# Cross attention queries of two heads as seven block products, beside the next head's keys and values

## The chip, the cores and the metric

The kernel runs on one core of a Trainium2 chip. The metric is the device time of one execution in microseconds (us); the time given for a kernel is the median of its runs.

## The reference

A decoder trunk of two layers over 512 tokens of width 1024, in float32. Each layer is a half-step SwiGLU FFN, a token mixer (differential attention in layer 0, a causal pooling mixer in layer 1), a cross attention of 4 heads into 256 memory tokens, and another half-step FFN; a layer norm follows each. The change touches the cross attention and the end of the pooling mixer.

```python
def memory_cross_attention(x, mem, wq, wkv, wo):      # x (1,512,1024), mem (1,256,1024)
    q = (x @ wq).reshape(B, S, XA_HEADS, XA_HEAD_DIM)  # 4 heads of 256
    k, v = jnp.split(mem @ wkv, 2, axis=-1)
    ...
    s = jnp.einsum('bshd,bmhd->bhsm', q, k).astype(jnp.float32) * (XA_HEAD_DIM ** -0.5)
    p = jax.nn.softmax(s, axis=-1).astype(v.dtype)
    o = jnp.einsum('bhsm,bmhd->bshd', p, v).reshape(B, S, D_MODEL)
    return o @ wo
...
x = layer_norm(a * x + memory_cross_attention(x, mem, xa_wq[i], xa_wkv[i], xa_wo[i]), ...)
```

## The kernel before

**Arithmetic.** Every float32 operand of a matmul is split into a high half (a rounded copy, `split`, line 114, on ScalarE = ACT) and a low half (operand minus high half, line 115, on VectorE = DVE, which so waits for ACT). One product is then three matmuls, `mm3` at lines 201 to 203: high by high, high by low, low by high. Weight tiles of 512 KB arrive by DMA issued on SyncE (SP) into a raw tile and are split into `wh` and `wl` in pieces of 128x1024; a raw tile may be loaded or added to again only when its two halves are made.

**FFN.** `up` computes its products two by two as seven block products in place of eight (a Strassen form): factors of x are made once by `second_factors` (lines 579 to 617), and the sums of weight blocks are made by DMAs that add into the raw tile in SBUF (`more`, line 636, `accum_op=ALU.add`, issued on GpSimd = POOL). Several units run in lanes, so that the additions to the tiles of one lane land while the others compute; between two uses of a raw tile stands one addition.

**Cross attention before.** `xa_main` goes head by head: keys `pk` and values `pv` of the head (`xa_kv`, 96 matmuls of 256 columns, results split into four tiles of the tag `kv`), then its queries `xq`: 48 matmuls of 512 columns (8 blocks of the inner dimension, two halves of the head's 256 columns, 3 matmuls each), 384 in the whole kernel. The raw weights are plain loads. `xa_side` (scores `xs`, softmax at lines 1290 to 1298, transposes, weighted sum `xo`, tile `oT`) is woven in by `weave`, 3 us of product time behind the head's queries. After that `to_tokens` multiplies by `wo` (`ps`) and adds into the rows X of the four token tiles, with the layer norm of each token tile: `ln_add` line 397, mean line 406 (DVE), square 419 (ACT), variance and reciprocal root `var`, `rstd` lines 420 and 421 (POOL), lines 423 and 425 (DVE), and then the transposes `pt` of its rows at line 479 (PE) with their split into `xh`, `xl`.

**Before the cross attention of layer 1** stands the pooling mixer: banded products `pp`, split into `pooled`, then `ps` and the layer norm. Beside it keys and values of head 0, after it those of head 1, are computed (`early_kv`), so that TensorE (PE) has work while the last token tiles are normalized.

**Order.** Each engine takes its instructions in a fixed order; a tile scheduler writes that order from the program and the priorities. An instruction that waits holds up what stands behind it on its engine. A DMA that POOL issues waits on POOL for the raw tile to be free.

Of the kernel before, what the change touches and what calls it, by code (L numbers as in the profile page):

```python
# [17 lines left out]
P = 128  # L18
D = 1024
S = 512  # L20
# [73 lines left out]
    return {"ident": ident, "mask": mask, "rope": rope, "band": band}  # L94


WAIT = object()


def drain(units):  # L100
    for _ in units:
        pass


class Trunk:
# [56 lines left out]
    @contextmanager  # L162
    def stage_pools(self, w, raw, order):

        with ExitStack() as ctx:
            self.stage = {}
            for n in order:
                if n == order[0]:
                    self.to_w(ctx)
                if n == "mem":  # L170
                    self.to_x(ctx)
                self.stage[n] = ctx.enter_context(self.pool(n))
            self.banks = {n: ctx.enter_context(self.pool(n, space=PSUM)) for n in ("px", "py", "yz")}
            self.w_bufs, self.raw_bufs, self.aux_turn = w, raw, 0
            self.w_order, self.raw_order = [("wh", "wl")], ["raw"]
            self.w_turn = self.raw_turn = 0
            yield
# [6 lines left out]

    def aux(self, name, tag=None):
        if tag is None:
            tag = list(self.banks)[self.aux_turn % 3]
            self.aux_turn += 1
        return self.banks[tag].tile([P, S], F32, tag=tag, name=name, bufs=2)

# [264 lines left out]
    def turn(self, t, half, two_pass=None):  # L455

        pt = self.aux("pt", "px" if "ra" in self.stage else None).rearrange("p (c n) -> p c n", c=4)
        c0 = half * S
        with self.behind() if self.last_mm else nullcontext():
            self.transpose4(pt, [self.X[t][:, c0 + j * P : c0 + (j + 1) * P] for j in range(4)])  # L460
        o = slice(t * P, (t + 1) * P)
        if self.ln_next == "ffn":
# [687 lines left out]
    def pool_mixer(self, layer, ln):  # L1150
# [32 lines left out]
            pooled.append(q)  # L1183
            yield
        wg = self.halves_wide(self.pool_w, "we", "we")
        self.w_order = [("wh", "wl")] * 3 + [("we", "we")] * 2
        self.raw_order = ["rawe"] * 3 + ["raw"] * 2
        self.begin_ln(layer, ln, 1.0)
        for t in range(NT):
            o = slice(t * P, (t + 1) * P)  # L1190
            for half in range(2):
# [12 lines left out]
                        )  # L1204
                self.ln_add(t, half, ALPHA, ps)
                yield
            self.turn_late()
            self.ln_token(t)


# [35 lines left out]
        for i, d in enumerate(self.kept):  # L1246
            self.nc.gpsimd.dma_start(self.mem_tile(2 * i), d)

    def xa_kv(self, w, h, ahead=None):
        nc = self.nc  # L1250
        rk = ahead or self.load_cols(w, h * 256)
        ps = self.mm("pk").rearrange("p (c n) -> p c n", c=2)
        for j in range(2):
            wk = rk[j] if ahead else self.halves(rk[j])
            for k in range(KC):
# [3 lines left out]
        kv = lambda: tuple(  # L1259
            self.kvp.tile([P, 2, MEM], F32R, tag="kv", name="kv", bufs=8) for _ in range(2)  # L1260
        )
        kt = kv()
        self.turn_late()
        self.split(kt[0], kt[1], ps)
        wv = self.halves_wide(self.load_wide(w, D + h * 256))
        ps = self.mm("pv").rearrange("p (m n) -> p m n", m=2)
        for m in range(2):
            o = slice(m * P, (m + 1) * P)
            for k in range(KC):
                mt = self.memT[k]  # L1270
                yield self.mm3(ps[:, m], (mt[0][:, o], mt[1][:, o]), wv[k], k == 0, k == KC - 1)
        v = kv()
        self.split(v[0], v[1], ps)
        return kt, v

    def xa_head(self, qs, kt, v):
        nc = self.nc
        pT = [self.pair("pT") for _ in range(2)]
        ps = []
        for tt in range(0, NT, 2):  # L1280
            sc = self.aux("xs").rearrange("p (t n) -> p t n", t=2)
            for i in range(2):
                o = slice((tt + i) * P, (tt + i + 1) * P)
                for c in range(2):
                    q = qs[c]
                    self.mm3(
                        sc[:, i], (q[0][:, o], q[1][:, o]), (kt[0][:, c], kt[1][:, c]), c == 0, c == 1
                    )
            mx, sm, rc = self.small("mx"), self.small("sm"), self.small("rx")
            nc.vector.tensor_reduce(mx, sc, AX.X, ALU.max, negate=True)  # L1290
# [10 lines left out]
        for tt in range(0, NT, 2):  # L1301
            p = ps[tt // 2]
            pt = self.aux("pt").rearrange("p (m i n) -> p m i n", m=2, i=2)
            for m in range(2):
                for i in range(2):
                    nc.tensor.transpose(pt[:, m, i], p[:, i, m * P : (m + 1) * P], self.ident)
            for m in range(2):
                o = slice(tt * P, (tt + 2) * P)
                self.split(pT[m][0][:, o], pT[m][1][:, o], pt[:, m].rearrange("p i n -> p (i n)"))
            yield  # L1310
        for c in range(2):
# [4 lines left out]
            o = self.pair("oT")  # L1316
            self.split(o[0], o[1], po)
            self.oT.append(o)
            yield

    def early_kv(self, layer, heads, ahead=None):
        for h in heads:
            self.kv.append((yield from self.xa_kv(self.a["xa_wkv"][layer], h, ahead)))

    def xa_main(self, layer):
        wq, wkv = self.a["xa_wq"][layer], self.a["xa_wkv"][layer]
        early = len(self.kv)
        for h in range(XA_H):
            if h >= len(self.kv):
                self.kv.append((yield from self.xa_kv(wkv, h)))  # L1330
            kt, v = self.kv[h]
            qs = []
            ws = [self.halves(lo) for lo in self.load_cols(wq, h * 256)]
            ps = [self.mm("xq") for c in range(2)]
            for p in ((0, 2 * P), (2 * P, S)) if self.late else ((0, S),):
                for c in range(2):
                    yield from self.project(ps[c], ws[c], (p,))
                    self.turn_late(1 - c)
            for c in range(2):
                q = self.pair("q")  # L1340
                self.split_scaled(q[0], q[1], ps[c], (D // XA_H) ** -0.5)
                qs.append(q)
            self.heads.append((self.clock, (qs, kt, v)))
            if 0 < early and h + early < XA_H:
                self.kv.append((yield from self.xa_kv(wkv, h + early)))
        yield from self.to_tokens(self.oT, self.a["xa_wo"][layer], 0, 4, True, False, ALPHA)

    def xa_side(self):
        for h in range(XA_H):
            while h >= len(self.heads) or self.clock < self.heads[h][0] + 3000:  # L1350
                yield WAIT
            yield from self.xa_head(*self.heads[h][1])

    def cross_attention(self, layer, ln):
        bufs = dict(q=8, oT=10, gb=2)
        if layer == 0:
            self.kv = []
            mem = self.side_pool("mem")
            with self.other_pools():
                self.stage["mem"] = mem  # L1360
                with self.phase_pool(("gb", "gb"), "p", pT=6, p=4, kv=8, _x=0, **bufs):
                    self.kvp = self.phase["kv"]
                    self.mem_tiles = []
                    with self.tc.high_priority():
                        self.turn_memory("p")
                    self.xa(layer, ln)
            self.close_side()
        else:
            with self.later, self.phase_pool(("gb", "gb"), "p", pT=6, p=4, **bufs):
                self.xa(layer, ln)  # L1370

    def xa(self, layer, ln):
        self.heads, self.oT = [], []
        self.weave(self.xa_main(layer), self.xa_side(), 2500)
        if layer == 0:
            self.keep_memory()
        self.begin_ln(layer, ln, 1.0)
        kv = lambda: tuple(self.kvp.tile([P, S], F32R, tag="kv", name="kv", bufs=8) for _ in range(2))
        homes = [[lambda: self.pair("q")] * 4, [kv] * 4]
        drain(self.to_tokens(self.oT[4:], self.a["xa_wo"][layer], 4, 4, False, True, ALPHA, homes))  # L1380


# [68 lines left out]
    def mixer(self, layer, ln):  # L1451
# [5 lines left out]
        else:  # L1457
            w = self.a["xa_wkv"][layer]
            self.later = ExitStack()
            self.later.enter_context(self.late_pools())  # L1460
            self.kvp = self.later.enter_context(self.pool("kv"))
            with self.phase_pool(("pooled", "pooled"), "sq", pooled=20, sq=1):
# [57 lines left out]
```

## Time and profile before

| | us |
|---|---|
| time, median of 3 runs | 1949.34 (1948.71 to 1950.73) |
| profiled execution, own time | 1952.38 |
| its span | 1950.6 |
| PE busy | 1918.7 (98%), 13052 matmuls |
| PE's weight loads busy | 1746.2 (90%) |
| DVE busy | 1560.5 (80%) |
| ACT busy | 1012.7 (52%) |
| POOL busy | 336.1 (17%) |
| cross attention of layer 0, on PE | 601.5 to 765.1 |
| pooling mixer and cross attention of layer 1, on PE | 1421.2 to 1614.5 |

The profiled execution took 1.8 us more than its span, and 3.0 us more than the median. In the timeline a row is start, duration, engine, line, operation, tile written, tiles read, shape and count; in square brackets the idle time before it and what ended that. Matmuls are pipelined: the distance of two starts is the pace, not the duration of one. PEclk is the share of TensorE's full clock that was granted.

### The profile page before, as it was taken

How to read it: one execution, taken by the hardware profiler on the slowest of the kernel's cores; microseconds unless marked ns; L12 is line 12 of the kernel's file. 1: busy time of each engine (PE TensorE's matmuls, PEld its weight loads, DVE VectorE, ACT ScalarE, POOL GpSimd, SP SyncE). 2: the span in 40 equal slices, each digit the busy share in tenths (PEclk: the TensorE clock that was granted, in tenths of full speed). 3: DMA queues.
4: the chain of work that ended last, by engine and by line, in shares of the span. 5: the costliest groups of instructions: out<-in, count | busy, mean ns of one | idle time of the engine just before them, and what ended most of it. 6: DMA issues, size and time to landing. Idle time of an engine off the chain costs nothing.

```text
span 1950.6 us, 32439 instructions
## 1 busy us (share of the span) xinstructions
PE 1918.7 (98%) x13052; PEld 1746.2 (90%) x13052; DVE 1560.5 (80%) x2200; ACT 1012.7 (52%) x1537; POOL 336.1 (17%) x317
## 2 busy tenths in 40 slices
PE   9999999999999999999999999999999999999998
PEld 8999998888778888989998999999888889999996
DVE  7988987788867557798887888888876468888886
ACT  6555553466655444555554555455445436555552
POOL 3212121111211002312210322112110013111211
PEclk9999999999999999999999999999999999999999
DMA  9888772322135325977695598778435336778861
GB/s 253 197 174 180 167 152 66 90 65 87 44 108 177 126 65 141 218 171 147 149 200 143 105 210 173 174 162 163 153 119 162 109 87 116 189 172 172 182 143 44
DMA packets 254182, 280.58 MB, mean 144 GB/s; under 512 B 9168, under 2 KB 221648, under 8 KB 254032
## 3 DMA queue, kind: packets, MB, share of 16 engines
q0 software_dynamic: 95808, 102.77, 32.4%
q1 hardware_dynamic: 158224, 175.74, 28.3%
q8 instruction: 102, 1.67, 0.3%
q14 instruction: 48, 0.39, 0.1%
HBM read 274.28 MB, written 4.20 MB: 143 GB/s over the span
## 4 chain that ended last, share of the span: by engine, by line
PE 79%; DVE 13%; ACT 3%; issue 3%; DMA 2%; POOL 1%; SPq 0%; DVEq 0%; POOLq 0%; ACTq 0%
PE x L201 7%; PE x L202 7%; PE x L203 7%; PE z L201 4%; PE z L202 4%; PE z L203 4%; PE ps L203 4%; PE ps L202 4%; PE ps L201 4%; DVE wl L115 3%; PE px L201 2%; PE px L203 2%; PE px L202 2%; PE y L203 2%; PE xq L201 2%
## 5 line engine op out<-in xcount | busy, mean ns | idle before, releaser
L636 POOL DMA_DIRECT2D ra<-in_ffn_w_in_dram x132 | 170.5, 1315 | 993.3 <-DVE wl L115 971.3
L114 ACT CAST wh<-ra 128x1024 fp32r<-128x1024 f32 x184 | 193.3, 1052 | 213.8 <-PE x L202 67.7
L115 DVE TENSOR_TENSOR wl<-ra,wh 128x1024 fp32r<-128x1024 f32 x184 | 223.6, 1220 | 70.8 <-ACT wh L114 64.7
L114 ACT CAST wh<-rc 128x1024 fp32r<-128x1024 f32 x136 | 142.9, 1053 | 120.6 <-PE x L202 45.5
L201 PE MATMUL x<-xh,wh 128*128 128x256 f32 x704 | 197.1, 280 | 1.5 <-ACT xh L114 0.8
L203 PE MATMUL x<-xh,wl 128*128 128x256 f32 x704 | 196.6, 279 | 1.9 <-DVE wl L115 1.9
L202 PE MATMUL x<-xl,wh 128*128 128x256 f32 x704 | 196.3, 279 | 0.0
L201 PE MATMUL x<-xe,wh 128*128 128x256 f32 x704 | 195.7, 278 | 0.0
L202 PE MATMUL x<-xe,wh 128*128 128x256 f32 x704 | 195.6, 278 | 0.0
L203 PE MATMUL x<-xe,wl 128*128 128x256 f32 x704 | 195.5, 278 | 0.0
L114 ACT CAST wh<-b 128x1024 fp32r<-128x1024 f32 x112 | 117.8, 1051 | 131.8 <-PE x L202 63.5
L115 DVE TENSOR_TENSOR wl<-rc,wh 128x1024 fp32r<-128x1024 f32 x136 | 164.4, 1219 | 22.9 <-ACT wh L114 22.9
L115 DVE TENSOR_TENSOR wl<-b,wh 128x1024 fp32r<-128x1024 f32 x112 | 136.7, 1221 | 41.6 <-ACT wh L114 41.6
L201 PEld LDWEIGHTS x<-xh,wh 128*128 128x128 f32 x704 | 133.0, 189 | 3.5 <-ACT xh L114 1.1
L203 PEld LDWEIGHTS x<-xh,wl 128*128 128x128 f32 x704 | 133.3, 189 | 2.4 <-DVE wl L115 2.4
L202 PEld LDWEIGHTS x<-xl,wh 128*128 128x128 f32 x704 | 133.4, 189 | 1.5 <-DVE xl L115 0.2
L201 PEld LDWEIGHTS x<-xe,wh 128*128 128x128 f32 x704 | 132.6, 188 | 1.4
L202 PEld LDWEIGHTS x<-xe,wh 128*128 128x128 f32 x704 | 132.5, 188 | 1.3
L203 PEld LDWEIGHTS x<-xe,wl 128*128 128x128 f32 x704 | 132.5, 188 | 0.0
L203 PE MATMUL y<-xh,wl 128*128 128x256 f32 x352 | 99.1, 281 | 2.1 <-DVE wl L115 1.2
L201 PE MATMUL y<-xh,wh 128*128 128x256 f32 x352 | 98.2, 279 | 0.1
L201 PE MATMUL z<-xe,wh 128*128 128x256 f32 x352 | 97.9, 278 | 0.0
(404 smaller groups left out, 6085.8 us busy)
## 6 DMA issues: line engine op xcount, KB each, us to landing
ra<-in_ffn_w_in_dram POOLq DMA_DIRECT2D x132, 512.0 KB, 6.9
rc<-in_ffn_w_in_dram SPq DMA_DIRECT2D x88, 512.0 KB, 6.2
b<-in_ffn_w_out_dram SPq DMA_DIRECT2D x60, 512.0 KB, 4.9
ra<-in_ffn_w_in_dram SPq DMA_DIRECT2D x44, 512.0 KB, 4.7
rc<-in_ffn_w_in_dram POOLq DMA_DIRECT2D x44, 512.0 KB, 7.5
b<-in_ffn_w_out_dram POOLq DMA_DIRECT2D x16, 512.0 KB, 13.0
raw<-in_da_w_qkv_dram SPq DMA_DIRECT2D x16, 512.0 KB, 5.1
raw<-in_xa_wkv_dram SPq DMA_DIRECT2D x8, 1024.0 KB, 5.4
```

What stands on the lines that cost most here:

```text
L114: self.nc.scalar.copy(hi, src),
L115: self.nc.vector.tensor_sub(lo, src, hi.bitcast(F32)),
L201: mm(out, w[0], x[0], start=start, stop=False, skip_group_check=again)
L202: mm(out, w[0], x[1], start=False, stop=False, skip_group_check=again)
L203: self.last_mm = mm(out, w[1], x[0], start=False, stop=stop, skip_group_check=again)
L636: self.last_more = nc.gpsimd.dma_start(t, source(*block), accum_op=ALU.add)
```

## The change

Queries of two heads are one unit of seven block products in the form of the FFN's `up`. `x_factors` makes the factors of x for it, `queries` the products; the sums of weight blocks are made by DMAs that add into three raw tiles: `ra` becomes W11, then +W12, then +W22; `rc` is W21, then has W22, W12 and W11 added to it, three times in a row; `rd` is W22, then +W12. The products have 256 columns. The heads' queries are complete only at the end of a unit. `xa_kv` gives control back at marks, and its parts are laid between the seven products, in layer 0 in the order (q, k) four times and then q three times, with keys and values of head 0 ahead; in layer 1's first unit k and q in turn, then three more q. Early keys and values of head 1 no longer stand between the pooling mixer and the cross attention of layer 1; that layer's first products stand there. Pools change with it: `kt` and `v` take the place of `kv`, `oT` lies in tiles `q`, six tiles `xe` hold factors and six tiles `q` the temporaries of `x_factors`, and layer 1 keeps 2 in place of 3 pairs `wh`, `wl`.

```diff
+    def x_factors(self):
+        nc, F, H = self.nc, self.factors, 2 * P
+        temps = [self.tmp("q", (P, 4, H)) for _ in range(6)]
+        s3, a11, a12, a21, s1, s2 = temps
+        def part(i, x, o):
+            self.split(F[i][0][:, :, o], F[i][1][:, :, o], x)
+        for r, (hi, lo) in zip((a11, a12), F):
+            nc.vector.tensor_tensor(r, hi.bitcast(F32), lo.bitcast(F32), ALU.add)
+        yield
+        for t in (2, 3):
...
+            nc.scalar.copy(b21, pts[0])
+            nc.vector.tensor_tensor(t1, pts[1], b21, ALU.subtract)
+            part(3, t1, o)
+            part(2, pts[1], o)
+            nc.vector.scalar_tensor_tensor(t2, t1, -1.0, a11[:, :, o], ALU.mult, ALU.subtract)
+            nc.vector.scalar_tensor_tensor(t1, t2, -1.0, a12[:, :, o], ALU.mult, ALU.subtract)
+            part(6, t1, o)
+            yield
+            part(4, t2, o)
+            nc.vector.tensor_tensor(t3, a11[:, :, o], b21, ALU.subtract)
+            part(5, t3, o)
+            yield
+    def queries(self, w, u, tags):
...
+        def more(t, *block):
+            nc.gpsimd.dma_start(t, source(*block), accum_op=ALU.add)
+        def product(ps, raw, a, start=False):
+            v, x = self.halves(raw), self.factors[a]
+            after(raw)
+            for j in range(2):
+                o = slice(j * P, (j + 1) * P)
+                for k in range(4):
+                    yield self.mm3(
+                        ps[:, j], (v[0][:, k, o], v[1][:, k, o]), (x[0][:, k], x[1][:, k]),
+                        start and j == k == 0, j == 1 and k == 3, True,
+                    )
...
+        ra = self.load([4, H], source(1, 1), tags[0])
+        rc = self.load([4, H], source(2, 1), tags[1])
+        yield MARK
+        after = lambda raw: more(raw, 1, 2)
+        x = bank(self.mm("xq"))
+        yield from product(x, ra, 0, True)
+        p1 = sums()
+        nc.scalar.copy(p1, x)
+        yield MARK
+        def after(raw):
+            for block in ((2, 2), (1, 2), (1, 1)):
+                more(raw, *block)
+        y = bank(self.aux("y", "yz"))
+        yield from product(y, rc, 1, True)
+        rd = self.load([4, H], source(2, 2), tags[2])
+        nc.vector.tensor_tensor(p1, y, p1, ALU.add)
+        qa = self.pair("q", (P, 2, S))
+        keep(qa, first, p1, 1)
+        yield MARK
+        after = lambda raw: more(raw, 2, 2)
+        z = bank(self.aux("z", "yz"))
+        yield from product(z, ra, 3, True)
...
+        after = lambda raw: more(raw, 1, 2)
+        yield from product(z, rd, 6)
+        yield MARK
+        after = lambda raw: None
+        yield from product(x, ra, 4)
...
+        yield from product(x, rd, 5)
...
+        yield from product(x, rc, 2)
+        keep(qa, second, x, 1)
+        self.heads += [(self.clock, qa), (self.clock, qb)]
+        yield MARK
     def xa_main(self, layer):
...
+        for u in range(XA_H // 2):
+            q = self.queries(wq, u, tags)
+            next(q)
+            k = self.xa_kv(wkv, u + 1, bank="yz")
+            next(k)
+            order = (k, q, k, q, k, q, k, q, q, q, q) if layer and not u else (q, k) * 4 + (q,) * 3
+            for g in order:
+                yield from step(g)
+                next(ready, None)
+        yield from whole(self.xa_kv(wkv, XA_H - 1))
...
+        homes = [
+            [lambda: [t[:, i] for t in (wide(),) for i in range(2)]] * 4,
+            [lambda: self.kv_pair("kt", [S])] * 2 + [lambda: self.kv_pair("v", [S])] * 2,
+        ]
+    def xa_pools(self):
+        order = ("wh", "wl", "kt", "raw", "rawe")
+        return self.stage_pools(dict(wh=4, wl=4), dict(raw=4, rawe=1), order)
     def late_pools(self):
-        order = ("wl", "wh", "raw", "rawe", "mem", "we")
-        return self.stage_pools(dict(wh=3, wl=3, we=4), dict(raw=2, rawe=3), order)
+        order = ("wl", "wh", "raw", "kt", "rawe", "we", "mem", "v")
+        return self.stage_pools(dict(wh=2, wl=2, we=4), dict(raw=2, rawe=3), order)
-                self.weave(self.early_kv(layer, (0,), ahead), side, 900, 6000)
-                drain(self.early_kv(layer, (1,)))
+                self.weave(whole(self.xa_kv(w, 0, ahead)), side, 900, 6000)
```

The order of instructions moves on every engine. First DVE in the cross attention of layer 0, from the low half of head 0's keys on (`kv`; `pk` and `pv` are products of keys and values, `xl` the low half of x, `wl` that of weights, `q` the queries). Before:

```order
L115 TENSOR_TENSOR kv_6850<-pk_6792,kv_6849 128x512
L115 TENSOR_TENSOR xl_6467<-pt_6865,xh_6465 128x4x128
L115 TENSOR_TENSOR xl_6468<-pt_6872,xh_6466 128x4x128
L115 TENSOR_TENSOR wl_6947<-raw_6944,wh_6946 128x1024
L115 TENSOR_TENSOR wl_6951<-raw_6944,wh_6950 128x1024
L115 TENSOR_TENSOR wl_7016<-raw_7012,wh_7015 128x1024
L115 TENSOR_TENSOR wl_7044<-raw_7012,wh_7043 128x1024
L115 TENSOR_TENSOR kv_6941<-pv_6891,kv_6940 128x512
```

And now the last 12 rows of the 23 that follow the low half of head 0's keys (`kt_6865`, now written ahead of all of them) up to `wl_7058`, the low half of `rc` = W21 (`q_6868` to `q_6873` are temporaries of `x_factors`, `xe` and `xl_6468` its results):

```order
L130 TENSOR_TENSOR xe_6798<-q_6872,xe_6795 128x4x128
L1376 TENSOR_TENSOR q_6872<-pt_7007,q_6871 128x4x128
L1384 TENSOR_TENSOR q_6868<-q_6869,q_6871 128x4x128
L130 TENSOR_TENSOR xe_6796<-q_6873,xe_6793 128x4x128
L130 TENSOR_TENSOR xl_6468<-q_6872,xh_6466 128x4x128
L130 TENSOR_TENSOR xe_6797<-q_6868,xe_6794 128x4x128
L130 TENSOR_TENSOR xl_6468<-pt_7007,xh_6466 128x4x128
L1379 SCALAR_TENSOR_TENSOR q_6873<-q_6872,q_6869 128x4x128
L130 TENSOR_TENSOR xe_6797<-q_6868,xe_6794 128x4x128
L1380 SCALAR_TENSOR_TENSOR q_6872<-q_6873,q_6870 128x4x128
L130 TENSOR_TENSOR xe_6796<-q_6873,xe_6793 128x4x128
L130 TENSOR_TENSOR wl_7058<-raw_6964,wh_7057 128x1024
```

Before, the low halves of query weights (`wl_6947`, `wl_6951`) stood third and fourth behind the keys'; now that of `rc`, which the second product reads, stands behind nearly all of `x_factors`.

POOL in the cross attention of layer 0 (`ra` of the rows before are weights of the FFN that follows). Before:

```order
L420 TENSOR_SCALAR var_6676<-var_6676 128x1
L421 TENSOR_TENSOR rstd_6677<-var_6676,mhalf_84 128x1
L636 DMA ra_8402<-in_ffn_w_in_dram 128x4x256
L636 DMA ra_8406<-in_ffn_w_in_dram 128x4x256
L636 DMA ra_8410<-in_ffn_w_in_dram 128x4x256
```

And now (`rawe_6962` is `ra`, `raw_6964` is `rc`, `raw_7088` is `rd` of unit 0):

```order
L436 TENSOR_SCALAR var_6676<-var_6676 128x1
L437 TENSOR_TENSOR rstd_6677<-var_6676,mhalf_84 128x1
L1400 DMA rawe_6962<-in_xa_wq_dram 128x4x256
L1400 DMA raw_6964<-in_xa_wq_dram 128x4x256
L1400 DMA rawe_6962<-in_xa_wq_dram 128x4x256
L1400 DMA raw_6964<-in_xa_wq_dram 128x4x256
L1400 DMA raw_7088<-in_xa_wq_dram 128x4x256
L1400 DMA raw_6964<-in_xa_wq_dram 128x4x256
```

Six adding transfers have come in, three of them into the one tile `raw_6964`.

POOL at the end of the pooling mixer of layer 1 (`var_15871` of before and `var_16118` of the change belong to token tile 0 of the norm ahead of the cross attention, the rows above them to the norm before the mixer). Before:

```order
L420 TENSOR_SCALAR var_15466<-var_15466 128x1
L421 TENSOR_TENSOR rstd_15467<-var_15466,mhalf_84 128x1
L420 TENSOR_SCALAR var_15871<-var_15871 128x1
L421 TENSOR_TENSOR rstd_15872<-var_15871,mhalf_84 128x1
L420 TENSOR_SCALAR var_15925<-var_15925 128x1
L421 TENSOR_TENSOR rstd_15926<-var_15925,mhalf_84 128x1
```

And now:

```order
L436 TENSOR_SCALAR var_15710<-var_15710 128x1
L437 TENSOR_TENSOR rstd_15711<-var_15710,mhalf_84 128x1
L1400 DMA raw_16308<-in_xa_wq_dram 128x4x256 x3
L436 TENSOR_SCALAR var_16118<-var_16118 128x1
L437 TENSOR_TENSOR rstd_16119<-var_16118,mhalf_84 128x1
L436 TENSOR_SCALAR var_16172<-var_16172 128x1
L437 TENSOR_TENSOR rstd_16173<-var_16172,mhalf_84 128x1
```

The three additions into `raw_16308` (`rc` of layer 1's first unit) have been put between the two norms.

More of the change, by code (lines that the diff above doesn't have):

```diff
@@ L102, in drain, with step, whole @@
         pass
+def step(units):
+    for ns in units:
+        if ns is MARK:
+            return
+        yield ns
+def whole(units):
+    for ns in units:
+        if ns is not MARK:
+            yield ns
 class Trunk:
@@ L1206, in pool_mixer @@
                 yield
-            self.turn_late()
+            if self.late and self.late[0] < 2:
+                self.turn_late()
             self.ln_token(t)
@@ L1325, in xa_main @@
     def xa_main(self, layer):
         wq, wkv = self.a["xa_wq"][layer], self.a["xa_wkv"][layer]
[L1327 to L1345, printed above, removed]
+        tags, keys = (("raw", "raw", "rawe"), ["rawe"]) if layer else (("rawe", "raw", "raw"), ["raw"])
@@ new lines, in xa_main @@
+        self.raw_order = keys
+        new = lambda: [self.act("xe", (P, 4, 2 * P)) for _ in range(3)]
+        self.factors = self.factor_views() + list(zip(new(), new()))
+        ready = self.x_factors()
+        if not layer:
+            k = self.xa_kv(wkv, 0)
+            next(k)
+            yield from step(k)
+            self.turn_late(2)
+            yield from step(k)
+        self.late = []
+        next(ready)
+        if not layer:
+            for _ in range(2):
+                yield from step(k)
+                next(ready)
```

128 lines of the change are left out of this document (87 added, 41 removed).

## The prediction

> **What bounds the kernel now.** I read the totals first, then the chain of work that ended last.
>
> ```profile
> span 1950.6 us, 32439 instructions
> PE 1918.7 (98%) x13052; PEld 1746.2 (90%) x13052; DVE 1560.5 (80%) x2200; ACT 1012.7 (52%) x1537; POOL 336.1 (17%) x317
> PE 79%; DVE 13%; ACT 3%; issue 3%; DMA 2%; POOL 1%; SPq 0%; DVEq 0%; POOLq 0%; ACTq 0%
> ```
>
> TensorE (PE) is the bound: fewer or shorter matmuls come off the end one for one, as long as nothing makes PE wait. So the question is how much PE time the products save, and what waits the new order brings. The windows of the two stages (columns: length, then busy time with instructions of PE, its weight loads, DVE, ACT, POOL; granted clock, DMA share, GB/s), and two short stretches in the second:
>
> ```profile
> 601.50:765.10 163.60, 162.69 (x979) 142.67 (x978) 99.30 (x155) 69.36 (x126) 10.59 (x10) 1.00 0.47 141
> 1421.20:1614.50 193.30, 188.27 (x1162) 167.81 (x1161) 126.22 (x207) 86.56 (x152) 17.76 (x19) 0.99 0.40 115
> 1452.00:1456.80 4.80, 2.77 (x22) 2.36 (x20) 4.75 (x12) 3.84 (x6) 0.74 (x2) 1.00 0.00 0
> 1456.80:1460.20 3.40, 3.15 (x15) 3.15 (x16) 2.95 (x6) 2.55 (x5) 0.18 (x1) 0.50 0.03 9
> ```
>
> Layer 0's stage has 0.91 us of PE idle, layer 1's 5.03: the change has little idle time to fill and much cover to lose. DVE is busy 99.3 of 163.6 us over the stage, but the change puts its new work into one place. The last two rows show a thing that waits can cost beside themselves: PE was busy 2.77 of 4.80 us, and then the clock was 0.50 for 3.4 us.
>
> **The products: -12 us.** Pace from starts in the timeline: first query matmul to first key matmul of the next head is 48 of 512 columns; first key matmul to first score, 48 of 256; first to last row of `z`, 72 of 256.
>
> ```profile
> 615.26 0.40 PE L201 MATMUL xq<-xh,wh 128*128 128x512 f32 x1
> 626.47 0.28 PE L201 MATMUL pk<-mem,wh 128*128 128x256 f32 x1
> 631.92 0.28 PE L201 MATMUL xs<-kv,q 128*128 128x256 f32 x1
> 1633.00 0.28 PE L201 MATMUL z<-xh,wh 128*128 128x256 f32 x1
> 1641.48 0.28 PE L201 MATMUL z<-xe,wh 128*128 128x256 f32 x1
> ```
>
> 11.21/48 = 0.2335 and 5.45/48 = 0.1135, 8.48/72 = 0.1178; I take their mean, 0.1157. Removed: 384 x 0.2335 = 89.7. Added: 7 products x 2 units x 2 layers x 24 = 672 matmuls, 77.7 (76.3 to 79.2). Gain 12.0 (10.5 to 13.4). A matmul of 256 columns costs 0.496 of one of 512, so seven eighths of the work is what remains.
>
> **A, VectorE in layer 0: +6.6.** `x_factors` puts 23 DVE rows between the low half of head 0's keys and that of `rc`: five of 1024 elements, eighteen of 512. None was there before; the nearest rows are those of `second_factors` and the splits, and two neighbours in the timeline for what a queue saves.
>
> ```profile
> L606 DVE TENSOR_TENSOR hb<-xh,xl x8: 1211/1218/1227, 11.7 to 1628.0; 128x1024 f32<-128x1024 f32 x8
> L600 DVE TENSOR_TENSOR b<-pt,b x8: 679/683/686, 16.0 to 1627.4; 128x512 f32<-128x512 f32 x8
> 606.97 1.22 DVE L115 TENSOR_TENSOR wl<-raw,wh 128x1024 fp32r<-128x1024 f32 x1
> 608.11 1.28 DVE L425 SCALAR_TENSOR_TENSOR X<-X,rstd,v 128x1024 f32<-128x1024 f32 x1
> 610.50 0.68 DVE L115 TENSOR_TENSOR kv<-pk,kv 128x512 fp32r<-128x512 f32 x1
> 607.68 1.04 PE L479 MATMUL pt<-ident,X 128*128 128x128 f32 x8
> ```
>
> Started back to back they stand 0.08 closer than they last (1.14 for 1.22): 5 x 1.22 + 18 x 0.68 - 23 x 0.08 = 16.5. The keys' low half ends at 611.2, so `rc`'s at 627.7. On PE, from the transposes at 607.68 to the third matmul of `y`, which reads it, the order has 101 matmuls and 16 transposes (0.1 each): 621.0. PE waits 6.7; I take 6.6. Down to 5.5 if the keys' low half takes the place that the order gives it (one 1.2 us earlier), up to 8 with ACT's casts, which stand before each low half.
>
> **B, three sums into one tile, layer 0: +9.5.** Each addition must wait for the landing of the one before. What one takes, in the whole trace and in its window from 155 to 185 us, with the issue row:
>
> ```profile
> L636 POOL DMA_DIRECT2D ra<-in_ffn_w_in_dram x132: 1274/1283/1733, 10.8 to 1875.6; - x132
> DMA to landing us min/median/max: 5.8/7.1/13.8
> DMA to landing us min/median/max: 6.0/9.2/10.0
> L114 ACT CAST wh<-ra 128x1024 fp32r<-128x1024 f32 x184 | 193.3, 1052 | 213.8 <-PE x L202 67.7
> 1438.43 0.59 ACT L114 CAST kv<-pv 128x512 fp32r<-128x512 f32 x1 [0.17 <-PE pv L203]
> ```
>
> No tile of before gets three in a row, so the sum is an estimate: 7.1 for the first, 9.2 for two beside other loads, 25.5. Then ACT casts `rc`, `v` and the next unit's `ra` in this order (1.05 + 0.59 + 1.05), and PE's `xq` of the next unit stands for the last. 627.7 + 25.5 + 2.7 = 655.9. PE, going on at 627.7, has 162 matmuls (18.7) before that: 646.4. Wait 9.5; at 5.8 each 1.4, at 9.2 each 11.6.
> [...]
>
> **C, start of the FFN behind each cross attention: +4.3 and +3.** The first FFN weight tile lies where `kt` lay, which the last products of `to_tokens` now read.
>
> ```profile
> 740.31 0.92 SPq L632 DMA_DIRECT2D ra<-in_ffn_w_in_dram  x2
> 762.28 0.48 PE L201 MATMUL ps<-kv,oT 128*128 128x512 f32 x1
> 765.13 0.28 PE L201 MATMUL x<-xh,wh 128*128 128x256 f32 x1
> ra<-in_ffn_w_in_dram SPq DMA_DIRECT2D x44, 512.0 KB, 4.7
> ```
>
> The load went 25 us ahead of its product; now it starts half way through the last group (763.7), lands 4.7 later, and is cast in 1.05: 769.5, against 765.13. That is 4.3 (3 to 5.8). For layer 1 I take 3 (0 to 4.3), since its pools lie otherwise.
>
> **D, POOL's queue in layer 1: +8.7.** Of `rc`'s three additions the second and third wait on POOL for a landing, and token 0's variance stands behind them.
>
> ```profile
> 1439.05 0.69 DVE L115 TENSOR_TENSOR kv<-pv,kv 128x512 fp32r<-128x512 f32 x1
> 1442.20 0.34 PE L201 MATMUL ps<-we,pooled 128*128 128x256 f32 x1
> 1447.70 0.75 POOL L420 TENSOR_SCALAR var<-var 128x1 f32<-128x1 f32 x1 [19.34 <-ACT sq L419]
> 1450.31 0.66 PE L479 MATMUL pt<-ident,X 128*128 128x128 f32 x4 [0.70 <-DVE X L425]
> ```
>
> In the order `rc`'s low half follows the values' (1439.05): 1440.9. Then 2 x 7.1 and an issue of 1.28: POOL is free at 1456.4, and the variance, wanted at 1447.70, comes 8.7 late; PE waits for that token already (0.70). With 5.8 each 6.1, with 9.2 each 12.9; the stretch from 1452 moves hardly any data (DMA share 0.00), so not the last.
>
> **E, VectorE in layer 1: +8.** From token 3's norm to the low half that `z` reads DVE has 23 rows, three of 1024: 3 x 1.22 + 20 x 0.68 - 23 x 0.08 = 15.4; PE has 63 matmuls and a few transposes, 7.7. 7.7 late, to 10 with ACT between; 8.
>
> **F, later sums, +1.5** (0 to 3.8): `ra`'s and `rd`'s last addition at the end of layer 1's first unit land after 7.1 to 9.2 and a cast, PE has 69 and 104 matmuls (8.0 and 12.0) meanwhile, so they come 0 to 2.3 late. **G, +3** (0 to 7): `rc` of the second units has 224 matmuls (26 us) against 3 x 7.1 to 3 x 9.2 and a cast, and two more low halves, 2.3 us, stand among `pooled`'s.
>
> **Clock: +4** (0 to 8). The longest single gap before the half clock was this:
>
> ```profile
> 1455.51 0.38 PE L201 MATMUL pk<-mem,wh 128*128 128x256 f32 x1 [1.24 <-ACT wh L241]
> ```
>
> After 2.03 idle us of 4.80 the half clock took 3.4 us, which is 1.7 of work lost. The waits B, C, D and E are of that size or longer; five (C twice) at 1.7 are 8.5, and I count half, since PE's next work may wait anyway: 4.
> [...]
>
> **Sum:** -12.0 + 6.6 + 9.5 + 4.3 + 3 + 8.7 + 8 + 1.5 + 3 + 4 = +36.6. The profiled execution took 1952.4, its span and 1.8 around it, 3.0 above the median of the runs; it would go to 1989.0, the median from 1949.3 to 1986. All covers that a wait uses up are counted once: PE resumes later, and so needs the next thing later.
>
> **The rivals.**
> R1, faster, 1937: the stage's length is PE's product count, and every new step hides: 1949.3 - 12. For it stands PE's 98%; against it that A follows from a fixed order and durations that hardly vary (679/683/686). It wins if the waits A to G come to less than 12 together, for which DVE's 23 rows would have to end before the second product, 6.6 us sooner.
> R2, slower by less, 1970: additions land in 5.8, the least seen. B 1.4, D 6.1, F 0, G 1, clock 2: -12 + 6.6 + 1.4 + 4.3 + 3 + 6.1 + 8 + 0 + 1 + 2 = +20.4. For it: the DMA share of 0.47 and 0.40 in the stages leaves room; against: half of all additions took over 7.1.
> R3, slower still, 2005: 9.2 each and a half clock behind every wait. B 11.6, C 5.8, D 12.9, F 3.8, G 7, C in layer 1 4, clock 8: -12 + 6.6 + 11.6 + 5.8 + 4 + 12.9 + 8 + 3.8 + 7 + 8 = +55.7. For it: 9.2 was measured where five came within 30 us, as here; against: layer 1's first ones fall where hardly any data moves.
>
> **How the numbers follow.** Forecast (1976 to 1996) 0.58, R2 (1960 to 1976) 0.20, R3 (above 1996) 0.12, R1 (below 1945) 0.07, waits that just eat the gain, about 1949, 0.03. A measurement of this kernel can tell 0.2%, 4 us, from no change. Faster 0.07, same 0.03, slower 0.90. The range leaves out R1, the case of no change and half of R3: 1962 to 2002.
>
> **What would show it.** Right: matmuls 13340; in layer 0 a wait of 5 to 8 us of PE for DVE at `y` and one at the next unit's `xq` that goes back to POOL's third addition; in layer 1 `pt` of token 0 waiting 7 to 9 us with POOL's variance behind three additions, and `z` waiting for `we`; the FFN's first product waiting for `ra`. Wrong: `y` starting without a wait, or additions into one tile landing closer than 5 us. A time under 1949 would say that PE had other work in these places than the order shows.

## The result, and the profile after

The changed kernel took 2009.24 us (median of 4 runs, 2005.75 to 2010.43) against 1950.03 of before on the same chip: 1.0301 times as long, 95% interval 1.0284 to 1.0319, or +59 us. The forecast was 1986, the range 1962 to 2002. The profiled execution took 2010.26 us, its span 2008.5, which is 57.9 longer than that of before.

The totals of the changed kernel, and the chain that ended last:

```profile
span 2008.5 us, 33208 instructions
PE 1934.9 (96%) x13340; PEld 1776.3 (88%) x13340; DVE 1603.4 (80%) x2256; ACT 1039.5 (52%) x1577; POOL 365.6 (18%) x341
PE 70%; DVE 15%; DMA 6%; ACT 4%; issue 3%; POOL 2%; SPq 0%; POOLq 0%; DVEq 0%; ACTq 0%
```

The matmuls are 13340, as forecast, and yet PE is busy 16 us longer with fewer columns to do: some of them ran slower. In the chain DMA has gone from 2% to 6%. The windows of the two stages (columns as in the prediction), between the same instructions as the windows of before:

```profile
602.46:784.27 181.81, 164.53 (x1123) 151.04 (x1120) 118.30 (x184) 79.44 (x144) 23.36 (x20) 0.96 0.55 138
1442.02:1669.45 227.43, 200.96 (x1306) 186.50 (x1304) 146.18 (x234) 100.33 (x174) 29.75 (x30) 0.89 0.46 112
```

Layer 0 went from 163.6 to 181.8 us, layer 1 from 193.3 to 227.4: +18.2 and +34.2. The FFN between them took 1.7 more, that behind layer 1 2.9 more, the start 1.0. The granted clock fell to 0.96 and 0.89. The waits of PE in the timeline, in order of time (in brackets the idle time and what ended it):

```profile
629.14 0.58 PE L219 MATMUL y<-xh,wl 128*128 128x256 f32 x1 [4.36 <-DVE wl L130]
643.99 0.38 PE L217 MATMUL z<-xe,wh 128*128 128x256 f32 x1 [2.63 <-ACT p L1445]
656.69 0.55 PE L217 MATMUL xq<-xh,wh 128*128 128x256 f32 x1 [4.15 <-ACT wh L129]
784.27 0.58 PE L217 MATMUL x<-xh,wh 128*128 128x256 f32 x1 [3.38 <-ACT wh L129]
1455.44 0.47 PE L1192 MATMUL pp<-bandh,xh 128*128 128x128 f32 x1 [3.28 <-ACT xh L129]
1487.87 0.66 PE L495 MATMUL pt<-ident,X 128*128 128x128 f32 x4 [2.71 <-DVE X L441]
1522.08 0.55 PE L217 MATMUL z<-xh,we 128*128 128x256 f32 x1 [8.16 <-ACT xe L129]
1540.59 0.41 PE L217 MATMUL xq<-xh,wh 128*128 128x256 f32 x1 [2.09 <-ACT wh L129]
1576.30 0.58 PE L217 MATMUL z<-xe,we 128*128 128x256 f32 x1 [3.51 <-ACT p L1445]
1672.31 0.39 PE L217 MATMUL x<-xh,wh 128*128 128x256 f32 x1 [1.97 <-DVE X L413]
```

Nearly every place that was named is there. With the short ones beside them, the idle times of PE of over 0.4 us are 18.0 us in layer 0's stage and 27.9 in layer 1's, each with the first products of the FFN behind it; in the trace of before 1.2 and 4.2. So waits make +40.5. Three rows tell what stands behind two of them: the third addition into `rc` in layer 0's first unit, the cast of `rc` that waits for it and holds up that of the next unit's `ra` (the 4.15 us), and the load of the first weight tile of the FFN behind layer 1, which came 38 us ahead of its product, so that the 1.97 us are not its doing:

```profile
645.72 1.27 POOL L1400 DMA_DIRECT2D raw<-in_xa_wq_dram  x1 [6.34 <-DMA raw<-in_xa_wq_dram]
654.16 1.04 ACT L129 CAST wh<-raw 128x1024 fp32r<-128x1024 f32 x1 [3.85 <-DMA raw<-in_xa_wq_dram]
1631.04 0.37 SPq L648 DMA_DIRECT2D ra<-in_ffn_w_in_dram  x1
```

The stretches at half clock in and right behind the two stages, three of eight, and the sum of all eight:

```profile
626.00:632.80 6.80, 3.66 (x17) 3.66 (x18) 6.80 (x9) 1.67 (x3) 1.59 (x2) 0.50 0.16 18
1455.50:1479.40 23.90, 23.29 (x108) 23.10 (x109) 10.74 (x15) 7.68 (x12) 1.97 (x2) 0.50 0.47 124
1516.90:1527.10 10.20, 4.67 (x19) 4.31 (x20) 10.20 (x16) 4.19 (x8) 0.89 (x1) 0.50 0.01 2
sum 71.50, PE 57.67 PEld 56.24 DVE 47.94 ACT 26.16 POOL 14.57; mean PE 7.21 PEld 7.03 DVE 5.99 ACT 3.27 POOL 1.82
```

71.5 us at half clock, with PE busy for 57.67 of them: at full clock that work would take about half (matmuls of 256 columns start 0.21 us apart in the stretches, 0.12 outside), so by estimate 28.8 us were lost; before it was 1.6, from the one stretch of 3.4 us in these stages. The sum: waits +40.5, clock +27.2, products -11 (below) make +56.7 of the 57.9.

The row from 1455.5 is the strange one. PE is busy 23.29 of 23.90 us and gets half the clock all that time. It begins with the end of the wait at `pp`, one of the first banded products of the pooling mixer, which the prediction didn't name.

### The profile page after: what moved, and what is told of

Read it like the earlier page. It is cut to its first block, busy times and chain, and to the rows that moved or that the text cites. A ratio compares the mean times of both kernels' runs of the same rounds, so it can differ in the third digit from the quotient of the medians.

```text
span 2008.5 us, 33208 instructions
## 1 busy us (share of the span) xinstructions
PE 1934.9 (96%) x13340; PEld 1776.3 (88%) x13340; DVE 1603.4 (80%) x2256; ACT 1039.5 (52%) x1577; POOL 365.6 (18%) x341
## 3 DMA queue, kind: packets, MB, share of 16 engines
q1 hardware_dynamic: 156368, 173.64, 27.2%
## 4 chain that ended last, share of the span: by engine, by line
PE 70%; DVE 15%; DMA 6%; ACT 4%; issue 3%; POOL 2%; SPq 0%; POOLq 0%; DVEq 0%; ACTq 0%
PE x L217 6%; PE x L218 6%; PE x L219 6%; PE z L217 4%; PE z L219 4%; PE z L218 4%; PE ps L219 3%; PE ps L218 3%; PE ps L217 3%; DVE wl L130 3%; DMA raw<-in_xa_wq_dram 2%; PE px L217 2%; PE px L219 2%; PE px L218 2%; PE y L219 2%
## 5 line engine op out<-in xcount | busy, mean ns | idle before, releaser
L219 PE MATMUL y<-xh,wl 128*128 128x256 f32 x376 | 106.4, 283 | 6.8 <-DVE wl L130 5.7
L217 PE MATMUL z<-xe,wh 128*128 128x256 f32 x376 | 104.6, 278 | 2.6 <-ACT p L1445 2.6
L217 PE MATMUL y<-xh,wh 128*128 128x256 f32 x376 | 105.6, 281 | 0.4 <-ACT wh L129 0.4
```

Source lines behind the costliest of these rows:

```text
L217: mm(out, w[0], x[0], start=start, stop=False, skip_group_check=again)
L219: self.last_mm = mm(out, w[1], x[0], start=False, stop=stop, skip_group_check=again)
```

## The experiments

My theory after the trace: the waits came about as predicted, and the missing 20 us are the clock, above all the stretch of 23.9 us, which a wait ahead of the pooling mixer set off. Rivals: the waits are all there is, and the low clock lies where PE would wait anyway; or VectorE's whole work is the limit of these stages, whatever its order. All kernels are the changed one with an edit, but for the ninth. Ratios are to the kernel before on the same chip; that of the change is 1.0301. Each is known to about 0.0018, or 3.5 us, so two edited kernels that lie less than some 5 us apart can't be told apart by their times.

**1. Work without a use ahead of the wait.** The edit, in the pooling mixer's products:

```diff
+                    if c == t == 0:
+                        for _ in range(44):
+                            mm(out, bandh[:, g, :P], bandh[:, g, :n], start=True, stop=True)
```

> 44 matmuls of 144 columns without a use, on operands that are long there, stand directly ahead of the first banded product of layer 1's pooling mixer, where PE waits 3.3 us in the changed kernel and after which the clock is 0.50 for 23.9 us; the result of the kernel is the same. Theory (the half clock, and not only the waits, makes the missing 20 us): the wait stays, the clock stays at 1.00 in that stretch, and the time falls by 8 to 12 us, to about 1999. Rival (the waits are all, the low clock only goes along with work that waits anyway): no change, or up to 1.5 us more where the added matmuls outlast the wait.

Measured: 1.0261 (1.0241 to 1.0280), 7.8 us less. The windows of the run, first over the banded products, then over the stretch that had been at half clock, and the transposes of token 0 behind it:

```profile
1451.40:1467.90 16.50, 16.50 (x149) 16.50 (x148) 12.90 (x16) 9.48 (x15) 2.61 (x3) 1.00 0.71 211
1455.50:1479.40 23.90, 19.69 (x172) 19.49 (x170) 14.48 (x24) 9.06 (x15) 2.64 (x2) 1.00 0.67 150
1483.02 1.12 PE L495 MATMUL pt<-ident,X 128*128 128x128 f32 x4 [7.82 <-DVE X L441]
```

The clock is 1.00 where it was 0.50, and the banded products end 16.3 us after their first start, fillers included, where they took 25.2. So 8.9 us came from the clock alone; nothing that PE waited for had been touched. Some was given back: token 0's transposes now wait 7.82 us in place of 2.71, since PE comes earlier and POOL doesn't. The rival falls here.

**2. The memory tiles back in their place.**

```diff
-        order = ("wl", "wh", "raw", "kt", "rawe", "we", "mem", "v")
+        order = ("wl", "wh", "raw", "kt", "rawe", "mem", "we", "v")
```

> In layer 1's pools the memory tiles go back to their place right behind rawe (the change had put the we tiles between). Theory: the memory loads then no longer start with those of the pooling weights at 1416 us but some 25 us earlier, as before the change; the pooling weights land 4 us sooner, DVE's norm behind them too, PE's 4.5 us of waits ahead of the first banded product go, and with them the half clock of 23.9 us: 12 to 16 us less, about 1995. Rival 1 (waits alone count): 4.5 us less, about 2005. Rival 2 (the place of the memory tiles is not what delays the pooling weights): no change.

Measured: 1.0259 (1.0241 to 1.0277), 8.2 us less. The first banded products of this run, and the transposes of token 0:

```profile
1449.95 0.33 PE L1192 MATMUL pp<-bandh,xh 128*128 128x128 f32 x1 [0.18 <-ACT xh L129]
1451.04 0.33 PE L1196 MATMUL pp<-bandh,xl 128*128 128x128 f32 x1 [0.76 <-DVE xl L130]
1476.69 1.12 PE L495 MATMUL pt<-ident,X 128*128 128x128 f32 x4 [7.51 <-DVE X L441]
```

The wait ahead of `pp` and the half clock are gone, and from the first key product of layer 1 to the first `ps` it is 20.8 us in place of 34.6: 13.8 less, the size expected. But 4.8 of it came back at the transposes, as in the first run. (The profile is of the fastest of four executions, 1998.98; the others took up to 2006.78.) The theory's place was right; that its gain would be passed on to the end was wrong.

**3. One sum in place of three.** `rc` needs W21 + W11 + W12 + W22, and `ra` at the end holds the last three:

```diff
-            for block in ((2, 2), (1, 2), (1, 1)):
-                more(raw, *block)
...
+            more(raw, 1, 2)
+            nc.gpsimd.dma_start(rc, ra, accum_op=ALU.add)
```

> The three additions into rc are replaced by one, of the finished ra (W11+W12+W22) from SBUF. Theory: the wait for rc at the end of layer 0's first unit (5.0 us) and POOL's block ahead of token 0's variance in layer 1 (2.7 us at the transposes) go, and a half clock of 6.8 us with the first: 8 to 12 us less, about 1999. Rival (the third addition is not what is waited for): under 3 us less. If the transfer out of SBUF lands late, a new wait stands at the last product of each unit.

Measured: 1.0210 (1.0191 to 1.0230), 17.7 us less, more than expected. In its profile token 0's transposes wait next to nothing. The next unit's first product in layer 0 waits 3.9 us (2.63 and a short one of 1.25) in place of 4.9, so that the 5.0 us of the theory did not go:

```profile
651.73 0.39 PE L217 MATMUL xq<-xh,wh 128*128 128x256 f32 x1 [2.63 <-ACT wh L129]
1481.99 0.66 PE L495 MATMUL pt<-ident,X 128*128 128x128 f32 x4 [0.77 <-DVE X L441]
```

The profile is of the slowest of its four executions (1999.5; the others took 1991.9 to 1993.0, at a granted clock of 0.985 to 0.987 against 0.981). The trace is 10.8 us shorter than that of the change, so these waits are shown, and the rest of the 17.7 only by the clock's mean. The half clock of 23.9 us is still in this trace.

**4. Factors in the products' order, `rc` split early.** The loops of `x_factors` over the two token tiles are cut in three: differences with the factors 3 and 2, then 6, then 4 and 5; and in `queries`:

```diff
+        early = None if u else self.halves(rc)
...
-        yield from product(y, rc, 1, True)
+        yield from product(y, rc, 1, True, early)
```

> x_factors makes its factors in the order in which the products want them (both tokens' third and fourth first), and the first unit's rc is split before the products start. Theory: in layer 0 y no longer waits for DVE (6.1 us) and no half clock follows (3.4 us lost), in layer 1 z waits less (8.2 us now) and so does the clock: 10 to 18 us less, about 1995. Rival (DVE's whole work up to z is the limit, not its order): 6 us less in layer 0, none in layer 1, about 2001.

Measured: 1.0269 (1.0243 to 1.0296), 6.2 us less, which is hardly clear of noise: its four executions took 1998.38 to 2009.57, and the profile is of one of 2009.52. So this run tells by its waits, not by its time. The waits in the places of 4.36 and 8.16:

```profile
629.11 0.58 PE L217 MATMUL z<-xh,wh 128*128 128x256 f32 x1 [7.71 <-ACT wh L129]
1530.21 0.58 PE L219 MATMUL z<-xh,we 128*128 128x256 f32 x1 [2.70 <-DVE we L130]
```

The wait of `y` on DVE is gone, so it was the order. But the time went to the next: with `rc` split first, its second addition stands on POOL ahead of `ra`'s first, and `z` waits for that. In layer 1 the wait fell from 8.16 to 2.70, so the order was the limit there too, and a new one of 5.93 stands at the transposes of token 3: DVE waited 6.09 us there for POOL's `rstd`, since the additions now stand ahead of that token's variance. Neither expectation gave that.

**5. `kt` behind the raw tiles in layer 0.** `order = ("wh", "wl", "raw", "rawe", "kt")`.

> In layer 0's pools the kt tiles stand behind raw and rawe, so that the FFN's first weight tile no longer lies where the last products of the cross attention read. Theory: the FFN's first product no longer waits (3.8 us at 781), and the half clock behind it (6.8 us from 783) goes too: 5 to 8 us less than the change. Rival (the wait alone counts): 3.8 less. Rival 2 (the load waits for something else): no change.

Measured: 1.0281 (1.0266 to 1.0296), 3.9 us less. The FFN's first product no longer waits, and no half clock follows there. By the trace the stage is 3.7 and the FFN behind it 1.2 shorter. The size is the rival's, but the interval can't tell it from the theory's 5 to 8. This run showed another thing: the same banded products, untouched, with the same wait of 3.28 us ahead of them, were at half clock for 10.2 us, not 23.9, and token 0's transposes then waited longer:

```profile
1449.90:1460.10 10.20, 9.80 (x46) 9.80 (x47) 4.82 (x7) 2.80 (x4) 0.00 (x0) 0.50 0.63 170
1481.34 1.11 PE L495 MATMUL pt<-ident,X 128*128 128x128 f32 x4 [8.51 <-DVE X L441]
```

**6. The four edits (2 to 5) together.**

> The four edits together: memory tiles back in place, one sum for rc, factors in the products' order with rc split early, kt behind raw. Theory (waits and the half clocks that follow them make all of the loss): the wait of 7.7 us that the third edit alone left at z in layer 0 stood behind rc's first addition and goes with the second edit; waits in both cross attentions fall from 46 us to about 20, half clocks from 72 us to about 25: near 1965, 45 less than the change. Rival (part of the loss is not in waits, DVE has too much work in these stages): 1980 or more, with DVE as releaser of the waits that are left.

Measured: 1977.13 us, 1.0130 (1.0113 to 1.0148), 33 less than the change. The windows of its stages:

```profile
601.03:775.66 174.63, 162.99 (x1123) 150.17 (x1122) 118.83 (x181) 81.16 (x145) 20.99 (x19) 0.97 0.55 136
1434.29:1636.04 201.75, 187.32 (x1305) 174.51 (x1304) 142.43 (x230) 99.36 (x172) 22.62 (x24) 0.97 0.43 115
```

Waits over 0.5 us are 27.1 us, not 20, and half clocks come to 24 us. The gain lies between the two expectations. The largest wait left was new, 7.3 us at the second unit's first product of layer 0: with one sum `ra`'s only tile is held until the transfer from SBUF has landed (7.4 us after its issue at 640.32), and the next unit's `ra` is loaded after that (issued at 647.84).

**7. Edits 2 and 3 alone.**

> Memory tiles back in place and one sum for rc, nothing else. With the clock kept at 1.00 token 0's transposes in layer 1 waited 7.5 us behind POOL's three additions; in the change only 2.7, since the half clock had made PE late as well. Theory: so the two edits gain more than the sum of what each gave alone in layer 1 (10.2 and 7.1): the wait of 7.5 goes whole, layer 1 falls by some 18 to 20, the kernel to about 1985. Rival (the gains overlap, since one stretch is paid by either): layer 1 falls by 12, the kernel to about 1993.

Measured: 1.0161 (1.0146 to 1.0177), 27 us less. The window of layer 1, and token 0's transposes:

```profile
1436.40:1641.37 204.97, 187.46 (x1306) 174.47 (x1304) 142.79 (x230) 99.04 (x172) 22.74 (x24) 0.96 0.43 114
1465.22 0.66 PE L495 MATMUL pt<-ident,X 128*128 128x128 f32 x4 [0.70 <-DVE X L441]
```

The time is near the theory's, and the rival falls. In the traces layer 1 fell by 22.5 us, where the two edits alone had given 10.2 and 7.1. That the two gain more together than the sum of each alone is not shown by this: the trace of run 3 is of its slowest execution, and by the times 8.2 and 17.7 alone stand against 27 together. What the traces show is that the half clock and POOL's block hide each other: with the half clock alone gone PE waits 7.51 us for POOL at token 0's transposes (run 2), with POOL's block alone gone it comes there late by the half clock and waits 0.77 (run 3), and in the change, which has both, it waits 2.71.

**8. Wide matmuls in the middle of the half clock.** Ahead of the third banded product (`c == 2`):

```diff
+                for _ in range(32 if c == 2 else 0):
+                    mm(pp[:, :256], bandh[:, g, :P], self.memT[0][0], start=True, stop=True)
```

> 32 matmuls of 256 columns without a use, 3.7 us at full and 7.5 us at half clock, stand in the middle of the banded products of layer 1's pooling mixer, where PE is never idle and yet the clock stays at 0.50 for 23.9 us; the result is the same. Theory (narrow matmuls of 16 to 144 columns do not count as enough work to bring the clock back, wide ones do): the clock returns to 1.00 inside or right behind them, the half clock there ends some 10 us sooner, and the time stays within 4 us of the change in spite of the added 7 us. Rival (the clock comes back after a fixed time or at the stage's end): the half clock lasts to the same instruction, and the time rises by 6 to 8 us.

Measured: 1.0315 (1.0297 to 1.0332), 2.7 us more than the change. The stretches before and after the clock's return:

```profile
1452.30:1459.10 6.80, 6.11 (x28) 6.11 (x29) 4.43 (x7) 2.29 (x4) 0.00 (x0) 0.50 0.46 138
1459.10:1470.20 11.10, 11.10 (x100) 11.10 (x98) 4.17 (x6) 4.31 (x7) 0.30 (x1) 1.00 0.44 127
```

The time can't be told from that of the change. The added matmuls start at 1458.49, and 0.6 us later the clock is 1.00. That is what the theory expects. But 6.8 us is also the commonest length of the stretches in the change, and run 5 got its clock back after 10.2 us without them, so that wide matmuls are needed is not shown.

**9. The kernel before, with the memory tiles put late.** One line of before: `order = ("wl", "wh", "raw", "rawe", "we", "mem")`.

> The kernel before, with one edit only: in layer 1's pools the memory tiles stand behind the we tiles, as in the change. Theory (this place alone delays the memory loads into those of the pooling weights and starts the chain of wait and half clock, without any of the new products): PE waits 3 to 5 us longer ahead of the banded products of the pooling mixer, a half clock of 6.8 us or more begins there, and the time rises by 6 to 14 us, to 1956 to 1964. Rival 1 (waits alone): 3 to 5 us more. Rival 2 (the memory tiles' place matters only beside the change's other pools): no change.

Measured: 1962.86 us, 1.0052 (1.0034 to 1.0070), 10 us more than before. The wait ahead of the banded products, and the stretch behind it:

```profile
1436.65 0.48 PE L1176 MATMUL pp<-bandh,xh 128*128 128x128 f32 x1 [3.35 <-ACT xh L114]
1435.90:1459.80 23.90, 22.54 (x104) 22.35 (x105) 9.20 (x14) 6.41 (x11) 0.00 (x0) 0.50 0.36 116
```

With no new product in the kernel, the place of four tiles makes a wait of 3.35 us (and two short ones, 1.22 and 0.61) and 23.9 us of half clock. In the trace the memory loads start at 1396.9 in place of 1369.0 to 1391.8, beside those of the pooling weights. The profile is of the slowest of four executions (1967.25; the others took 1958.67 to 1964.36). This is shown by itself, then: a layout edit, 4.5 us of waits, 10 us of time.

**10. As 6, but `rc`'s sum by VectorE.**

```diff
+        after = lambda raw: nc.vector.tensor_tensor(rc, rc, raw, ALU.add)
         yield from product(x, ra, 4)
```

> As the run with all four edits, but rc's sum is one VectorE addition of ra to rc (1.2 us) in place of a transfer from SBUF, which took 7.5 us there and held ra's tile so long that the next unit's ra was loaded late. Theory: the wait of 7.3 us at the next unit's first product in layer 0 and the 3.2 us at the fifth in layer 1 go, with a half clock of 6.8 us: 8 to 14 us less than with four edits, near 1966. Rival (the next unit's ra is late for another reason): within 3 us of 1977. Neither expects it below the kernel before.

Measured: 1.0126 (1.0109 to 1.0143) against 1.0130 of run 6: no difference that can be told. The theory falls. The wait at the next unit's first product went from 7.32 to 2.26, but layer 0's stage only from 174.6 to 173.9, and the 3.2 us at layer 1's fifth product stayed (3.02). A wait of 2.34 at `pv` for DVE has come in, and ACT, which casts in a fixed order, stands 6.14 us for `rd`'s addition (issued at 635.6, landed at 645.3) with the casts of `rc`, `v` and the next `ra` behind it.

## Why the prediction was wrong, point by point

- **Products, -12.** Between starts at full clock, without idle times, the xq matmuls of before were 0.2355 apart on the mean, those of the change 0.1185 (538 of them): 90.4 - 79.6 = 10.8. Right.
- **A, +6.6.** 0.46 + 0.81 + 0.42 + 4.36 = 6.05 us, released by DVE but for the 0.81 (ACT). Right, and run 4 shows that the order on DVE was the cause.
- **B, +9.5.** 4.9 us (4.15 + 0.79). Right in place and cause, half in size: the second and third addition were each issued behind the landing of the one before (POOL waited 3.01 and 6.34 us for it), and the three took 24.5 us from the first issue to the cast behind the last, 25.5 was forecast, but PE came later than I had it, mainly by the 2.63 us at `z` and by the half clock from 626.
- **C, +4.3 and +3.** In layer 0 3.8 us (3.38 + 0.46): right, and run 5 takes it away by the cause named. In layer 1 2.6 (1.97 + 0.64), but there the size was luck: `ra` was issued at 1631.04 and cast at 1656.26, long before its product, and PE waited for rows of the norm and a low half on DVE.
- **D, +8.7.** 2.7 in the change, but 7.5, 7.8 and 8.5 in the runs in which PE got there at a better clock, and 0.7 in run 7 with the additions out of the way. In the change POOL waited 4.76 and 4.78 us for landings, and token 0's variance started at 1486.20, behind the third issue at 1484.85. The mechanism and the price were right, and hidden under the half clock.
- **E, +8.** 8.16, and 8.0 to 8.2 in all runs that kept the order; 2.7 to 3.4 where it was changed. Right in place, size and cause, the order on DVE. The row that `z` first stood for was not the low half of `we`, which came only at 1525.5, but one before it in that order: ACT's cast of `xe` (ended 1521.99) or DVE's addition of `y` (1521.93), which the trace can't tell apart.
- **F and G, +4.5.** F came as 3.5 us at the end of layer 1's first unit: 0.76 for `ra`'s last sum, and 2.73 (2.09 + 0.64) for the next unit's `ra`, which was loaded only when the halves of that sum were made (issued at 1535.69). G did not come. Two other places were missed: `z`'s second product waits for ACT's copy of its first result, which stands behind a cast that waits for an addition (2.63 and 3.51); and the 5.1 us ahead of and in the first banded products (1.21 + 3.28 + 0.61).
- **Clock, +4.** This is the step that failed: the half clock behind the waits cost 27.2 us (71.5 us of it, with 57.67 us of work). "five (C twice) at 1.7 are 8.5, and I count half" took 3.4 us for each wait, from the one stretch that I had quoted. In the change only one of eight stretches was so short; five lasted 6.8, one 10.2, one 23.9.

Waits were forecast at 44.6 us and came to 40.5. That these are so close is in part luck: the places that were named gave 31.8 us, and the missed ones, 2.63, 3.51 and 5.1, made up for most of the rest. The clock alone takes the time out of the range, and 11.6 of its 27 us (half of 23.29) come from the one stretch whose trigger the prediction didn't have: the diff moves `mem` behind `we` in one line of the pools, and of the pools it priced only where the FFN's tiles lay. Of the rivals R3 had the clock at 8 and the time nearest, 2005, for the wrong reason: landings of 9.2 us were not what was missing. (The row with the 9.2 counts four additions, not five.)

The clock in both traces is 1.00 or 0.50, and the eight stretches of the change are, to 0.1 us, one, two, three or seven times 3.4 us long. Waits of 2.0 to 4.4 us went with seven of them, the one of 8.16 with the eighth, and in the longest the clock stayed at 0.50 with PE busy for 23.29 of 23.90 us. The length of the wait alone does not give that of the half clock: 4.36 us went with 6.8, 3.28 with 23.9.

What stays open: why the stretch lasted 23.9 us in the change and in runs 3, 4 and 9 and 10.2 in run 5, and what in the narrow matmuls keeps the clock low, if they do. The traces show two things that bear on it. The four long stretches all ended 2.0 to 2.7 us behind the first `ps`, when the banded products were done. And in these four the clock had fallen before the wait ahead of the banded products ended, or with its end (0.71 us before to 0.03 behind); in run 5 it fell 0.66 us behind that end and came back after 10.2 us, in run 8 0.41 behind it and came back after 6.8. So the moment at which it falls may decide the length, and the added matmuls of run 8 may have had no part in it; neither was tested.

Runs 6 and 10 are the best of the new form, 25 us above before. Per layer the seven products bring some 5.4 us, and even in run 6 the waits over 0.5 us come to 10 us (layer 0) and 12 us (layer 1) more than before. The kernel before is the fastest that ran.

## What to carry to other kernels

Where TensorE is 98% busy, the cover that a change uses up is worth more than the products it saves: 11 us were saved, and waits of 40 us came in, most of them where the order on an engine, or the place of a tile in the pools, set when something else came. Price a new wait together with the clock that follows it: here waits of 40 us cost another 27. And two delays that end at the same instruction hide each other: in runs 1, 2 and 5, where the half clock ahead of token 0's transposes was gone or shorter, 4.8 to 5.8 us more of waiting for POOL came up there. So look at what stands behind a delay before counting on its removal.

## What the runs showed of the hardware

- A wait of 3.3 us ahead of narrow matmuls (16 to 144 columns, with some of 256 between) was followed by 23.9 us at half clock in four traces (the change, runs 3, 4 and 9), though PE was busy for 22.5 us or more of it, by 10.2 in run 5, and by 6.8 in run 8, where wider matmuls were put in; 44 matmuls without a use in that wait kept the clock at 1.00 for the same work.
- In the change the half clock that went with waits of 2.0 to 4.4 us ahead of matmuls of 256 columns lasted 3.4 or 6.8 us, that with the 8.16 us wait 10.2, half of it inside the wait (4.67 us of work in it).
- Twelve adding transfers of 512 KB out of SBUF landed 4.6 to 7.4 us after their issue, median 5.5 (runs 3, 6 and 7), the 24 out of HBM in the change 5.6 to 12.8, median 7.3; the same sum on VectorE took 1.23 us (run 10).
